# A depthwise convolution shared among four engines: four taps of two channel tiles become TensorE products with diagonal weights

## The chip, the cores and the metric

The kernel runs on one core of one Trainium2 chip. The metric is the device time of the whole program in microseconds (us). TensorE (PE in the profile) multiplies matrices and writes its sums to PSUM; VectorE (DVE), ScalarE (ACT) and GpSimd (POOL) work elementwise, and GpSimd doesn't reach PSUM; SyncE (SP) issues transfers. Each engine takes its own instructions in order and waits for others by semaphores.

## The reference, cut to what matters

A two-layer encoder on two sequences of 256 tokens with 1024 features, in fp32. Each layer has a mixer and a feed-forward part, each followed by a residual sum and a layer normalization. The first mixer is neighbourhood attention with a spatial gating unit. The second one is latent attention beside a gated convolution over time; the convolution has 31 taps, one weight per tap and channel, 512 channels:

```python
def dwconv(x, w, b):
    K, C = w.shape
    y = lax.conv_general_dilated(x, w[:, None, :].astype(x.dtype), window_strides=(1,),
                                 padding=[(K // 2, K // 2)],
                                 dimension_numbers=('NWC', 'WIO', 'NWC'),
                                 feature_group_count=C)
    return y + b.astype(x.dtype)
...
    c = latent_attention(c_q, c_kv, k_r, q_norm_g, w_uq, kv_norm_g, w_ukv, cos, sin)
    d = glu_a * jax.nn.sigmoid(glu_g)
    d = jax.nn.silu(layernorm(dwconv(d, conv_w, conv_b), conv_ln_g, conv_ln_b))
    return jnp.concatenate([c, d], axis=-1) @ w_out
```

The feed-forward part widens to 5632 features, has a convolution of three taps, gates, and narrows again to 1024.

## The kernel before, in words

The 512 tokens of both sequences are worked on together. Dense products split each fp32 operand into a rounded part and a rest ("hi" and "lo"), and take three products (hi x hi, hi x lo, lo x hi); `wload` (L105) loads a piece of weights and makes the two parts, the first on ScalarE (L109), the second on VectorE (L111). Products of plain fp32 operands, as the scores of the second mixer (`score`, L688), go to TensorE as they are; the trace has two records for each of them.

The order of the first layer is mixer, feed-forward; then comes `odd_mixer` (L532), the second mixer, and its feed-forward part. In `odd_mixer`:

- `glu(i)` (L536) makes channel tile i (of four, 128 channels each) of the convolution's input: two dense products of 24 steps each, then `gate(i)` (L546) under a raised priority. The gate takes the sigmoid on ScalarE (L551; for tiles 2 and 3 a tiny exponential behind it at L553 brings ScalarE's table for the softmax), multiplies on VectorE (L554) into `dpad[i]`, which holds both sequences with 15 zeros on either side, and begins two partial sums: `accps[i]`, a PSUM bank, with tap 0 and the bias on VectorE (L557), and `acc2`, in SBUF, with tap 21 on ScalarE (L559).
- `cproj`, `chain`, `kvproj`, `qproj` (L575 to L680) make the latent rows, normalize and transpose them (L622), and project keys, values and queries.
- `attend(p)` (L682) is attention for a pair of heads: for each sequence scores on TensorE, then for each head a maximum on VectorE (L491), exponentials with their sum on ScalarE (L494), a reciprocal on VectorE (L497), scaling (L501, on ScalarE; for the last pair L503, on VectorE), transposes on TensorE (L508), a copy out (L510), and the product with the values (L517) one step later. The exponentials lie in `er`, a `Ring` of two buffers, which makes four slots.
- L715 to L725 are the rest of the convolution. For each tile, VectorE adds taps 1 to 20 onto `accps[i]` (L719), one instruction a tap; for taps 22 to 30 ScalarE makes a scaled copy (L723, `pr`) and GpSimd adds it onto `acc2` (L724); VectorE adds the two sums at the end (L725).
- `conv_ln` (L727) transposes, normalizes over channels, transposes back (L748), applies SiLU and splits the result (L115, L116) into `mixT[4]` to `mixT[7]`; `OutProj` multiplies with the output weights, attention's half (`first`) before the convolution's half (`second`).

The order on each engine isn't the order of the code. The framework plans it from a timeline of estimated durations and priorities: what is ready and stands early in the code, or under a raised priority, goes first, and the rest of the convolution, which stands behind attention in the code, is filled in between. SBUF comes from pools with a fixed number of buffers: `act` has 30 of 4 KB per partition, `tmp` has 8; a new tile waits until a buffer is given back. PSUM has pools pA (4 banks), pB and pC (2 each). `Ring` (L77) takes `act` buffers and sets one element of each by a VectorE memset (L81).

Of the kernel before, what the change touches and what calls it, by code (L numbers as in the profile page):

```python
# [11 lines left out]
AF = mybir.ActivationFunctionType  # L12
# [3 lines left out]
P = 128  # L16
D = 1024
KC = 8
S = 256
# [4 lines left out]
RMS_EPS = 1e-6  # L24
NPAIR = 22
NPOOL = 10
NWARM = 18
ACUT = 832
KEEP = {4: 0, 7: 1, 10: 2, 13: 3}
# [20 lines left out]
def tile_encoder(ctx: ExitStack, tc: tile.TileContext, I, O):  # L50
# [26 lines left out]
    class Ring:  # L77
# [6 lines left out]
        def get(self):  # L84
            j = self.i % (2 * len(self.t))
            self.i += 1
            return self.t[j // 2][:, j % 2, :].rearrange("p (a k) -> p a k", a=2)

    def bank(pool, s="ps"):
        return pool.tile([P, 512], F32, tag="b", name=nm(s))  # L90
# [441 lines left out]
    def odd_mixer(xT):  # L532
# [13 lines left out]
        def gate(i, pa, pg):  # L546
            sg = tmp([P, 512], s="sig")
            d = dpad[i]
            out, va = d[:, :, 15:15 + S], pa.rearrange("p (s t) -> p s t", s=2)
            vs = sg.rearrange("p (s t) -> p s t", s=2)  # L550
            nc.scalar.activation(out=sg, in_=pg, func=AF.Sigmoid)  # L551
            if i >= 2:
                preload(AF.Exp, sg[:, 0:1])  # L553
            nc.vector.tensor_tensor(out=out, in0=va, in1=vs, op=ALU.mult)  # L554
            accps[i] = bank(pA, "cacc")
            a, a2 = accps[i].rearrange("p (s t) -> p s t", s=2), acc2[i // 2][:, i % 2]
            nc.vector.tensor_scalar(out=a, in0=d[:, :, 0:S], scalar1=pc("cw", i * 32),  # L557
                                    scalar2=pc("cw", i * 32 + 31), op0=ALU.mult, op1=ALU.add)
            nc.scalar.activation(out=a2, in_=d[:, :, 31 - NPOOL:31 - NPOOL + S], func=AF.Copy,  # L559
                                 scale=pc("cw", i * 32 + 31 - NPOOL))  # L560

        for i in range(4):
            d = act([P, 2, S + 30], s="dpad")
# [4 lines left out]
        for a in acc2:  # L568
            nc.gpsimd.memset(a[:, 0, 0, 0:1], 0.0)
        pr_ring = Ring(1, "pr")  # L570
        rope = const.tile([P, 2, 2, 32], F32, name="rope")
        after_mm(nc.gpsimd.dma_start(out=rope, in_=I["rope"]), last_mm[0])
        G = {"start": last_mm[0]}
# [107 lines left out]

        def attend(p):  # L682
            if p == 0:
                G["ring"] = Ring(2, "er"), Ring(2, "PTr")
            er, PTr = G["ring"]
            qT, kT = G["qT"][p], G["kT"][p]

            def score(out, qs, ks):  # L688
                for h in range(2):
                    mm(out[h], qT[:, h, qs], kT[:, h, ks], True, True)  # L690
            mixT[p] = act([P, 2, T], F32R, "mixT")
            if p == 2:
                G["sink"] = ToFeat(xscr[1], 1, last_mm[0], "ln1_g1", "ln1_b1", xscr[2], ())
            attention(p, score, G["V"], mixT[p], lambda ps, h, e: ps, er, PTr, p < 3, p == 3)
# [19 lines left out]
        op.first(0, (0, 1))  # L714
        for i in range(4):  # L715
            a, a2 = accps[i].rearrange("p (s t) -> p s t", s=2), acc2[i // 2][:, i % 2]
            for j in range(1, 31 - NPOOL):
                with tc.issue_after(G["cT_lo"].ins) if i == 0 and j >= 18 else nullcontext():
                    nc.vector.scalar_tensor_tensor(out=a, in0=dpad[i][:, :, j:j + S], scalar=pc("cw", i * 32 + j),  # L719
                                                   in1=a, op0=ALU.mult, op1=ALU.add)  # L720
            for j in range(32 - NPOOL, 31):
                pr = pr_ring.get()
                nc.scalar.activation(out=pr, in_=dpad[i][:, :, j:j + S], func=AF.Copy, scale=pc("cw", i * 32 + j))  # L723
                nc.gpsimd.tensor_tensor(out=a2, in0=a2, in1=pr, op=ALU.add)  # L724
            nc.vector.tensor_tensor(out=a2, in0=a, in1=a2, op=ALU.add)  # L725
# [196 lines left out]
```

## Time and profile before

| what | value |
|---|---|
| median of 3 runs | 1106.43 us (1104.14 to 1106.67) |
| the profiled execution | 1104.76 us, its span 1102.9 us |
| TensorE busy, span | 1082.3 us, 98% |
| VectorE busy | 673.2 us, 61% |
| ScalarE busy | 488.7 us, 44% |
| GpSimd busy | 226.6 us, 21% |
| mean granted clock of TensorE | 0.992 |

The span is what lies between the first and the last record of the profiled execution; its own time is 1.86 us longer. A busy share is an average over stages with different limits, so a stage is read from a stretch of its own. The granted clock is given as a share of 2.4 GHz.

### The profile page before, as it was taken

Reading aid. Unit: us, or ns where it says so; the run is one execution under the profiler, and the core shown is the slowest. Engines: PE = TensorE matmul, PEld = TensorE weight load, DVE = VectorE, ACT = ScalarE, POOL = GpSimd, SP = SyncE. Lnnn points to the kernel's source line nnn. Section 1 sums busy time; section 2 is a strip of 40 time slices with the busy share of each in tenths; the row PEclk is TensorE's granted clock in tenths of the full one; section 3 lists DMA queues with packets and bytes.
Section 4 is the critical chain, followed back from the end, with each engine's and each line's share of the span. In section 5 each row is a group of like instructions: output and inputs, shape, how many; then the busy total and the mean of one; then the engine's idle time right before and its main releaser. Section 6 shows DMA issues by size and latency. Waiting matters only on the chain.

```text
span 1102.9 us, 13655 instructions
## 1 busy us (share of the span) xinstructions
PE 1082.3 (98%) x5210; PEld 900.8 (82%) x5210; DVE 673.2 (61%) x996; ACT 488.7 (44%) x783; POOL 226.6 (21%) x222
## 2 busy tenths in 40 slices
PE   9999999999999999999999979999999999999996
PEld 7888778988888888888898856899888888888885
DVE  5378955766565656422578999587665656542227
ACT  5436644544444444421266797355444444431110
POOL 0482001200000000005464661830000000000173
PEclk9999999999999999999999979999999999999999
DMA  7852223533333323645232104254333333222602
GB/s 256 244 141 77 60 103 107 163 105 96 96 96 96 96 96 99 206 166 180 80 122 58 38 20 153 66 172 122 100 96 96 96 96 96 96 96 96 215 34 76
DMA packets 36098, 124.21 MB, mean 113 GB/s; under 512 B 4289, under 2 KB 5057, under 8 KB 36033
## 3 DMA queue, kind: packets, MB, share of 16 engines
q1 hardware_dynamic: 28864, 100.05, 29.5%
q0 software_dynamic: 6448, 22.53, 6.0%
q8 instruction: 41, 0.67, 0.3%
q10 hardware_dynamic: 720, 0.75, 0.2%
q14 instruction: 25, 0.20, 0.1%
HBM read 113.88 MB, written 8.39 MB: 111 GB/s over the span
## 4 chain that ended last, share of the span: by engine, by line
PE 93%; DVE 3%; ACT 2%; issue 1%; DMA 0%; POOL 0%; POOLq 0%; DVEq 0%; ACTq 0%
PE up L95 44%; PE dn L95 29%; PE qk L95 4%; PE op L95 4%; PE glu L95 3%; PE v L95 2%; PE u L95 2%; PE s L95 1%; PE pv L95 1%; PE pt L508 1%; DVE cacc L719 1%; PE lnT L237 1%; DVE wlo L111 1%; DVE qT L655 0%; ACT er L494 0%
## 5 line engine op out<-in xcount | busy, mean ns | idle before, releaser
L95 PE MATMUL up<-xT,whi 128*128 128x512 f32 (+1 forms) x1536 | 439.9, 371 | 0.0
L111 DVE TENSOR_TENSOR wlo<-raw,whi 128x1024 fp32r<-128x1024 f32 (+1 forms) x174 | 238.8, 1374 | 297.4 <-ACT whi L109 296.1
L95 PEld LDWEIGHTS up<-xT,whi 128*128 128x128 f32 x1536 | 279.9, 188 | 49.9
L109 ACT CAST whi<-raw 128x1024 fp32r<-128x1024 f32 (+1 forms) x174 | 182.4, 1050 | 249.1 <-PE dn L95 132.6
L95 PE MATMUL up<-xT,wlo 128*128 128x512 f32 (+1 forms) x768 | 284.0, 372 | 0.0
L95 PE MATMUL dn<-whi,gT 128*128 128x512 f32 x704 | 217.4, 389 | 0.0
L95 PEld LDWEIGHTS up<-xT,wlo 128*128 128x128 f32 x768 | 144.4, 188 | 24.9
L95 PEld LDWEIGHTS dn<-whi,gT 128*128 128x128 f32 x704 | 132.0, 188 | 27.2
L95 PE MATMUL dn<-wlo,gT 128*128 128x512 f32 x352 | 136.9, 389 | 0.0
L186 POOL DMA_DIRECT2D xres<-xscr x12 | 6.5, 546 | 576.0 <-PE dn L95 576.0
L95 PEld LDWEIGHTS dn<-wlo,gT 128*128 128x128 f32 x352 | 66.1, 188 | 13.8
L115 ACT CAST gT<-cv 128x512 fp32r<-128x512 f32 x44 | 27.3, 620 | 111.6 <-DVE cv L782 111.6
L771 ACT ACTIVATE cv<-up,par 128x512 f32<-128x512 f32 x88 | 68.3, 776 | 0.0
L774 DVE SCALAR_TENSOR_TENSOR cv<-up,par,cv 128x510 f32<-128x510 f32 x88 | 65.8, 748 | 2.7
L781 ACT ACTIVATE cv<-cv 128x512 f32<-128x512 f32 x44 | 27.8, 632 | 85.2 <-DVE cv L774 85.2
L772 DVE SCALAR_TENSOR_TENSOR cv<-up,par,cv 128x510 f32<-128x510 f32 x88 | 65.4, 743 | 0.0
L719 DVE SCALAR_TENSOR_TENSOR cacc<-dpad,par,cacc 128x512 f32<-128x512 f32 x80 | 58.9, 750 | 1.1
L724 POOL TENSOR_TENSOR acc<-acc,pr 128x512 f32<-128x512 f32 x36 | 48.7, 1353 | 38.9 <-ACT pr L723 32.2
L116 DVE TENSOR_TENSOR gT<-cv,gT 128x512 fp32r<-128x512 f32 x44 | 30.4, 692 | 27.5 <-ACT gT L115 27.5
L95 PE MATMUL op<-whi,mixT 128*128 128x512 f32 x128 | 44.3, 402 | 0.0
L95 PE MATMUL dn<-whi,mixT 128*128 128x512 f32 x128 | 42.8, 394 | 0.0
L95 PE MATMUL glu<-xT,khi 128*128 128x512 f32 (+1 forms) x160 | 42.0, 349 | 0.0
(195 smaller groups left out, 1351.4 us busy)
## 6 DMA issues: line engine op xcount, KB each, us to landing
raw<-in_wup SPq DMA_DIRECT2D x88, 512.0 KB, 3.6
raw<-in_wdn SPq DMA_DIRECT2D x44, 512.0 KB, 3.5
raw<-in_wout SPq DMA_DIRECT2D x16, 512.0 KB, 3.7
xscr<-xres POOLq DMA_DIRECT2D x12, 512.0 KB, 3.7
xres<-xscr POOLq DMA_DIRECT2D x12, 512.0 KB, 4.4
raw<-in_wqk SPq DMA_DIRECT2D x8, 512.0 KB, 6.6
raw<-in_wglu SPq DMA_DIRECT2D x8, 512.0 KB, 3.8
raw<-in_wug SPq DMA_DIRECT2D x7, 512.0 KB, 3.6
```

The source lines that it names most:

```text
L95: last_mm[0] = nc.tensor.matmul(out=out, lhsT=lhsT, rhs=rhs, start=first, stop=last)
L109: nc.scalar.copy(out=hi[:, :n], in_=raw[:, :n])
L111: nc.vector.tensor_tensor(out=lo[:, :n], in0=raw[:, :n], in1=hi[:, :n].bitcast(F32), op=ALU.subtract)
L115: nc.scalar.copy(out=dst[:, 0, sl], in_=src)
L116: nc.vector.tensor_tensor(out=dst[:, 1, sl], in0=src, in1=dst[:, 0, sl].bitcast(F32), op=ALU.subtract)
L237: nc.tensor.transpose(self.banks[k // 2][:, (k % 2) * S + q * P:(k % 2) * S + q * P + P], x[:, k * P:(k + 1) * P], ident)
L719: nc.vector.scalar_tensor_tensor(out=a, in0=dpad[i][:, :, j:j + S], scalar=pc("cw", i * 32 + j), in1=a, op0=ALU.mult, op1=ALU.add)
L724: nc.gpsimd.tensor_tensor(out=a2, in0=a2, in1=pr, op=ALU.add)
L771: nc.scalar.activation(out=c, in_=pv, func=AF.Identity, scale=pc(fw, ch * 4 + 1), bias=pc(fw, ch * 4 + 3))
L772: nc.vector.scalar_tensor_tensor(out=c[:, :, 1:S], in0=pv[:, :, 0:S - 1], scalar=pc(fw, ch * 4), in1=c[:, :, 1:S], op0=ALU.mult, op1=ALU.add)
L774: nc.vector.scalar_tensor_tensor(out=c[:, :, 0:S - 1], in0=pv[:, :, 1:S], scalar=pc(fw, ch * 4 + 2), in1=c[:, :, 0:S - 1], op0=ALU.mult, o ...
L781: nc.scalar.activation(out=cg, in_=cg, func=AF.Silu)
```

## The change

For channel tiles 2 and 3, taps 27 to 30 become four products on TensorE. Their weights are diagonal matrices, one for each tile and tap, in a new tile `taps` that GpSimd makes at the start of the second mixer by multiplying the identity with the taps' weights. The four products go into the bank `accps[i]` inside `gate(i)`, in place of the VectorE instruction that began this sum; tap 0 becomes one more step of VectorE's chain, and the bias moves into ScalarE's first tap, whose function is Identity with a bias instead of Copy. ScalarE and GpSimd lose four taps of each of the two tiles: 22 to 26 are left. The buffers for the exponentials of the second mixer are taken from the pool `tmp`, one at a time, instead of a ring of two `act` buffers. Tiles 0 and 1 are as before, but for the function's name at L559, which is Identity with a bias of 0.

```diff
--- before.py
+++ after.py
@@ -24,6 +24,7 @@
 RMS_EPS = 1e-6
 NPAIR = 22
 NPOOL = 10
+NTAP = 4
 NWARM = 18
 ACUT = 832
 KEEP = {4: 0, 7: 1, 10: 2, 13: 3}
@@ -85,6 +86,10 @@
             j = self.i % (2 * len(self.t))
             self.i += 1
             return self.t[j // 2][:, j % 2, :].rearrange("p (a k) -> p a k", a=2)
+
+    class Loose:
+        def get(self):
+            return tmp([P, 512], s="e").rearrange("p (a k) -> p a k", a=2)
 
     def bank(pool, s="ps"):
         return pool.tile([P, 512], F32, tag="b", name=nm(s))
@@ -554,10 +559,15 @@
             nc.vector.tensor_tensor(out=out, in0=va, in1=vs, op=ALU.mult)
             accps[i] = bank(pA, "cacc")
             a, a2 = accps[i].rearrange("p (s t) -> p s t", s=2), acc2[i // 2][:, i % 2]
-            nc.vector.tensor_scalar(out=a, in0=d[:, :, 0:S], scalar1=pc("cw", i * 32),
-                                    scalar2=pc("cw", i * 32 + 31), op0=ALU.mult, op1=ALU.add)
-            nc.scalar.activation(out=a2, in_=d[:, :, 31 - NPOOL:31 - NPOOL + S], func=AF.Copy,
-                                 scale=pc("cw", i * 32 + 31 - NPOOL))
+            if i < 2:
+                nc.vector.tensor_scalar(out=a, in0=d[:, :, 0:S], scalar1=pc("cw", i * 32),
+                                        scalar2=pc("cw", i * 32 + 31), op0=ALU.mult, op1=ALU.add)
+            else:
+                for n in range(NTAP):
+                    mm(a, taps[:, i - 2, n, :], d[:, :, 31 - NTAP + n:31 - NTAP + n + S], n == 0, n == NTAP - 1)
+            nc.scalar.activation(out=a2, in_=d[:, :, 31 - NPOOL:31 - NPOOL + S], func=AF.Identity,
+                                 scale=pc("cw", i * 32 + 31 - NPOOL),
+                                 bias=pc("cw", i * 32 + 31) if i >= 2 else 0.0)
 
         for i in range(4):
             d = act([P, 2, S + 30], s="dpad")
@@ -568,6 +578,11 @@
         for a in acc2:
             nc.gpsimd.memset(a[:, 0, 0, 0:1], 0.0)
         pr_ring = Ring(1, "pr")
+        taps = act([P, 2, NTAP, P], s="taps")
+        for i in range(2):
+            o = PCOL["cw"][0] + (i + 2) * 32 + 31 - NTAP
+            nc.gpsimd.tensor_tensor(out=taps[:, i], in0=ident[:, None, :].broadcast_to([P, NTAP, P]),
+                                    in1=par[:, o:o + NTAP, None].broadcast_to([P, NTAP, P]), op=ALU.mult)
         rope = const.tile([P, 2, 2, 32], F32, name="rope")
         after_mm(nc.gpsimd.dma_start(out=rope, in_=I["rope"]), last_mm[0])
         G = {"start": last_mm[0]}
@@ -681,8 +696,8 @@
 
         def attend(p):
             if p == 0:
-                G["ring"] = Ring(2, "er"), Ring(2, "PTr")
-            er, PTr = G["ring"]
+                G["ring"] = Ring(2, "PTr")
+            er, PTr = Loose(), G["ring"]
             qT, kT = G["qT"][p], G["kT"][p]
 
             def score(out, qs, ks):
@@ -714,11 +729,11 @@
         op.first(0, (0, 1))
         for i in range(4):
             a, a2 = accps[i].rearrange("p (s t) -> p s t", s=2), acc2[i // 2][:, i % 2]
-            for j in range(1, 31 - NPOOL):
+            for j in range(1 if i < 2 else 0, 31 - NPOOL):
                 with tc.issue_after(G["cT_lo"].ins) if i == 0 and j >= 18 else nullcontext():
                     nc.vector.scalar_tensor_tensor(out=a, in0=dpad[i][:, :, j:j + S], scalar=pc("cw", i * 32 + j),
                                                    in1=a, op0=ALU.mult, op1=ALU.add)
-            for j in range(32 - NPOOL, 31):
+            for j in range(32 - NPOOL, 31 if i < 2 else 31 - NTAP):
                 pr = pr_ring.get()
                 nc.scalar.activation(out=pr, in_=dpad[i][:, :, j:j + S], func=AF.Copy, scale=pc("cw", i * 32 + j))
                 nc.gpsimd.tensor_tensor(out=a2, in0=a2, in1=pr, op=ALU.add)
```

## Rows read from the trace of the kernel before

**Rows 1.** The page, part 1: busy us of each engine, share of the span, instructions.

```profile
PE 1082.3 (98%) x5210; PEld 900.8 (82%) x5210; DVE 673.2 (61%) x996; ACT 488.7 (44%) x783; POOL 226.6 (21%) x222
```

**Rows 2.** Stretches of the second mixer: length, busy us PE, PEld, DVE, ACT, POOL; granted clock.

```profile
612.00:641.00 29.00, 29.00 (x133) 24.14 (x133) 27.39 (x40) 21.84 (x40) 17.55 (x13) 1.00 0.19 55
630.00:641.00 11.00, 11.00 (x54) 9.25 (x53) 10.59 (x14) 7.74 (x19) 9.42 (x7) 1.00 0.33 96
641.00:660.00 19.00, 11.78 (x41) 7.28 (x40) 17.19 (x32) 18.33 (x42) 10.44 (x9) 0.64 0.01 1
644.50:658.00 13.50, 9.48 (x27) 5.53 (x28) 13.09 (x24) 13.47 (x33) 9.56 (x8) 0.50 0.01 2
660.00:682.00 22.00, 20.42 (x120) 14.50 (x119) 20.83 (x47) 20.08 (x63) 5.28 (x9) 1.00 0.46 168
682.00:742.00 60.00, 59.98 (x343) 50.32 (x342) 42.36 (x79) 26.99 (x48) 31.29 (x22) 1.00 0.34 105
```

**Rows 3.** Timeline of TensorE: start us, us, what, how often, [idle before, releaser].

```profile
638.31 0.39 PE L95 MATMUL glu<-xT,klo 128*128 128x512 f32 x1
...
640.70 0.60 PE L508 MATMUL pt<-ident,er 128*128 128x128 f32 x4
647.50 2.07 PE L95 MATMUL s<-kT,qT 128*128 128x256 f32 x4 [6.20 <-ACT er L494]
...
709.80 0.39 PE L95 MATMUL op<-whi,mixT 128*128 128x512 f32 x1
```

**Rows 4.** Groups of instructions, shapes apart, 545 to 742: count | busy us, mean ns | idle.

```profile
L719 DVE SCALAR_TENSOR_TENSOR cacc<-dpad,par,cacc 128x512 f32<-128x512 f32 x80 | 58.9, 750 | 1.1
L724 POOL TENSOR_TENSOR acc<-acc,pr 128x512 f32<-128x512 f32 x36 | 48.7, 1353 | 38.9 <-ACT pr L723 32.2 <-issue 4.9
...
L723 ACT ACTIVATE pr<-dpad,par 128x512 f32<-128x512 f32 x36 | 25.2, 723 | 5.6 <-POOL acc L724 5.6
...
L557 DVE TENSOR_SCALAR cacc<-dpad,par 128x512 f32<-128x512 f32 x4 | 3.2, 810 | 0.0
```

**Rows 5.** Timeline of VectorE, columns as in rows 3.

```profile
569.73 0.06 DVE L81 MEMSET pr<- 128x1 f32 x1 [3.26 <-PE glu L95]
...
588.38 0.55 DVE L610 TENSOR_TENSOR craw<-ra,rb 128x128 f32<-128x128 f32 x1
...
622.89 0.69 DVE L554 TENSOR_TENSOR dpad<-glu,sig 128x512 f32<-128x512 f32 x1
...
629.66 3.81 DVE L111 TENSOR_TENSOR wlo<-raw,whi 128x1024 fp32r<-128x1024 f32 x2
...
634.05 0.68 DVE L491 TENSOR_REDUCE nmx<-s 128x2 f32<-128x512 f32 x1
...
642.44 0.69 DVE L554 TENSOR_TENSOR dpad<-glu,sig 128x512 f32<-128x512 f32 x1 [1.41 <-ACT sig L551]
...
706.49 1.27 DVE L116 TENSOR_TENSOR mixT<-cb,mixT 128x512 fp32r<-128x512 f32 x2
```

**Rows 6.** Groups of ScalarE's instructions, 634 to 682, columns as in rows 4.

```profile
L723 ACT ACTIVATE pr<-dpad,par 128x512 f32<-128x512 f32 x12 | 8.5, 726 | 1.5 <-POOL acc L724 1.5
```

**Rows 7.** Chain of waits that ended last: start us, us, engine, tile, line, how often.

```profile
586.57 8.65 PE glu L95 x38
595.22 1.31 PE dn L622 x12
...
651.86 2.07 PE s L95 x4
...
660.36 0.86 PE s L95 x4
```

**Rows 8.** Timeline of GpSimd, columns as in rows 3.

```profile
575.52 4.03 POOL L724 TENSOR_TENSOR acc<-acc,pr 128x512 f32<-128x512 f32 x3 [4.86 <-issue]
```

**Rows 9.** Timeline of ScalarE in the first mixer and its output's normalization.

```profile
98.36 1.28 ACT L494 ACT_TABLE_LOAD   x1
...
185.79 3.76 ACT L246 ACTIVATE xv<-lnT,par 128x256 f32<-128x256 f32 x8
```

**Rows 10.** Timeline of ScalarE at the end of attention in the second mixer.

```profile
685.85 0.47 ACT L494 ACTIVATE er<-s,nmx 128x256 f32<-128x256 f32 x1 [3.30 <-DVE nmx L491]
```


## The prediction

> **What bounds the kernel now.** I read the page's totals first: TensorE is busy for 98% of the span, 1082.3 us [rows 1], so nearly all work added to it must find one of its few gaps. Next I cut the second mixer into stretches [rows 2]. The reader should see three stages there. From 612 to 641 us TensorE has no gap. From 641 to 660 it is busy for 11.78 of 19 us at a mean granted clock of 0.64, and from 660 to 682 for 20.42 of 22. After 682 it is full again, and the feed-forward that follows fills it to the end. So time is won or lost in this mixer by how much of TensorE's waiting between 641 and 682 remains, less what is added to its work.
>
> How large is that loss? Idle time is 7.22 + 1.58 = 8.8 us [rows 2]. From 644.5 to 658 us the granted clock is 0.50, 1.2 of 2.4 GHz, and there the engine is busy for 9.48 us [rows 2], of which half, 4.7 us, would go at the full clock. That makes 13.5 us.
>
> Who makes it wait? The gap of 6.20 us before a score product ends on ScalarE's exponential [rows 3]. From 641 to 660 ScalarE is busy for 18.33 of 19 us and from 660 to 682 for 20.08 of 22; VectorE for 17.19 and 20.83 [rows 2]. Attention is paced by ScalarE, with VectorE, which squeezes the convolution in between, close behind.
>
> **The change part by part.** *Taps taken off ScalarE and GpSimd.* Tiles 2 and 3 drop from nine scaled copies to five each. Eight copies of 0.72 us leave ScalarE and eight adds of 1.35 us, 10.8 us, leave GpSimd [rows 4]. GpSimd ends nothing here, so its relief counts for nothing; a VectorE split that runs slower beside it would gain at most tenths, since the pair at 629.66 [rows 5] still meets the adds that remain. On ScalarE only copies that stand in its full stretch count, from 634 on. Twelve stand there [rows 6], the last three of tile 2 and the nine of tile 3. Five of tile 2 and five of tile 3 stay, those of tile 2 all before 634, so of the twelve five stay and seven go. A copy's record of 0.72 us overlaps the next one by some 0.1, so I price it at 0.63, an estimate. Gain: 7 x 0.63 = 4.4 us of ScalarE.
>
> *VectorE.* The first tap of tiles 2 and 3, a TENSOR_SCALAR of 0.81 us, becomes a 0.75 us step of the chain [rows 4], and two memsets go: 0.2 us in all. The number of steps stays, 21 per tile. So VectorE is not relieved; it can only use its idle time, 1.81 us between 641 and 660 and 1.17 up to 682, and 0.41 before 641 (11.00 less 10.59, from 630 on) [rows 2], together 3.4 us. That caps the gain at 3.4 us, unless chain steps slip past the end of attention. I take the cap.
>
> *Products on TensorE.* Eight products of 512 fp32 columns. The trace has fp32 products of 256 columns: four records, which are two products, in 0.86 us at the full clock and 2.07 at half [rows 7], so 0.43 and 1.03 us each. With twice the columns a tap costs 0.86, four 3.4, eight 6.9 us at the full clock. Where do they lie? Tile 2's become ready when VectorE has made their input, about 623.6 [rows 5]; TensorE is full then, with q products and the last gated unit's, up to 638.7 [rows 3]. They push these 3.4 us later, into the gap that starts at 641. The pushed gate of tile 3 is not urgent for VectorE, which still has steps of tile 2 to do. The q products feed VectorE steps that are over when its two splits begin at 629.66; attention's first maximum comes only at 634.05, after them [rows 5]. Those 3.8 us of splits cover the push. Cost 0, and 3.4 us if the cover fails. Tile 3's four come once VectorE has made its input, 643.1 in the trace of before and a little later now. They fall into the 6.2 us gap, or delay the scores behind them: cost 0 to 3.4 us. I take 0, the gap being the nearest row. Check: 13.5 less 6.9 less 3.4 leaves 3.2 us of loss over 41 us, which is the rate of 660 to 682 (1.58 in 22). The sum is possible, but nothing larger is, without a better clock.
>
> *What waits behind a tap.* TensorE takes its queue in order, so until the gate's product on VectorE lands, scores and transposes behind the taps stand still. VectorE itself waited 1.41 us there for the sigmoid [rows 5]. That much could come on top; bound 0 to 1.4, taken 0, since TensorE idled through that wait already.
>
> *Diagonals.* Two GpSimd products over 512 columns, about 1.35 us each like the adds of that size, 2.7 us, fit the 4.86 us in which GpSimd idles before its first adds [rows 8]. They take a buffer of a full pool of thirty: the memset before them waited 3.26 us for one [rows 5]. The tile for the second sequence's latent rows, first written at 588.38 [rows 5], may then wait until half of gated unit 1 is through (24 products from 586.57 on, 0.228 each by 38 in 8.65: 592.0), 3.6 us later, and the transposes at 595.22 [rows 7], which need it, come late by at most as much. TensorE has the 48 products of gated unit 2 to do meanwhile: 0, bound 3.6. The scratch tiles for exponentials come from eight slots instead of four: 0, or a few tenths of gain.
>
> *Bias in the first ScalarE tap.* An Identity with a bias in place of Copy. Could it force a table load, 1.28 us? After the load for the exponential at 98.36 the same function with bias ran at 185.79 with no load between [rows 9]. Cost 0.
>
> *After 682.* TensorE needs the convolution's output at 709.80; VectorE's last write of it is at 707.7, 2.1 us ahead [rows 3, 5]. The transposes, ScalarE's function and these writes follow TensorE's order and move up with it, up to the cap taken. The sum: 1104.76 for the profiled execution (span 1102.9 and 1.86 around it) less 3.4 is 1101.4. The median of the runs shown stands 1.67 above that execution, so **1103.0 us** against 1106.43.
>
> **Rivals.** *VectorE holds it.* It is busy 95% of 660 to 682; its steps are as many as before, and if order and latency use up its idle time again, attention ends when it did and the eight products only fill gaps. For: the steps of cacc, 0.75 us each, stand before every maximum, and the last exponential, at 685.85, had waited 3.30 us for VectorE's [rows 10]. Against: they have no due time before the output projection. Gain 0 to 1.5, say 0.7: 1105.7.
>
> *The products stand in the way* (slower). Place: TensorE's queue, at 623.6 and 645. Price: four products 3.4 us before q, and four more between gate and scores, each time with ScalarE starved as long. It decides if attention's first scores move by more than VectorE's two splits hide, 3.8 us: from there each us of push is a us of the end. Price with relief partly kept: 6.9 less 3.4, plus 3.5 us: 1109.9. With only one burst uncovered it is 0. For: TensorE is full from 612 to 641 [rows 2]. Against: ScalarE has copies to do during the bursts.
>
> *The clock holds.* The granted clock fell to 0.50 after TensorE had stopped at 641.3, and rose again near 658, after products had run from 647.5 [rows 2, 3]. With 3.4 us of gated products pushed to 644.7 and tile 3's taps to 648.5, the long gap may not form at all, and scores, transposes and values that took twice their time would cost ScalarE less waiting: up to 4.7 us more, of which 3.2 is left to win by the check above: 1103.0 - 3.2 = 1099.8. The Trainium skill, "TensorE: Matmul & The Clock Gate", in its Part 1 says the full clock is a state that activity releases and idling takes back; by it this case would be the likeliest and the time near 1100. Here the trace agrees on the fall, but it has no stretch of mixed short products that shows the clock held. Against the rival: each tap waits for VectorE, so a gap stays before it.
>
> *It does not do what it says:* the planner may place the taps late, at the end of tile 2's chain, so that VectorE idles for them. Then 2 to 4 us are lost; I count this with the slower case.
>
> **How the numbers follow.** The sum's own case gets 0.45, and its bounds (from -5 to about -1 us) put 0.25 of that at faster and 0.20 at same. About 0.3%, 3.3 us, is what a measurement can tell from no change. The clock's case gets 0.15, all faster. VectorE's case gets 0.17, all same. The products in the way get 0.23, of which 0.20 slower and 0.03 same. Faster 0.40, same 0.40, slower 0.20. The range goes from the clock's case, 1099.5, to just short of the worst of the slower case, 1109.0: beyond it lies about a fifth.
>
> **What would show it.** Right: eight fp32 products of 512 columns near 624 to 649, records of 0.43 us apart and two per product; ten copies in place of eighteen for tiles 2 and 3; the last exponential before 683 instead of 685.85; TensorE's waits between 641 and 682 down from 8.8 to about 3 us. Wrong: a wait of TensorE on dpad longer than 1.5 us, VectorE idle in front of the chain of tile 2, first scores after 633, or the convolution's last add later than in the trace of before. The forecast fails on the good side if the clock is 1.00 all through.

## The result and the profile after

The changed kernel takes 1122.54 us (median of four runs, 1122.16 to 1124.79) against 1105.29 for the kernel before beside it: ratio 1.0167, interval 1.0155 to 1.0179. That is 17.2 us slower. The forecast was 1103.0 us with a range up to 1109.0, so both its sign and its range were wrong. The profiled execution took 1122.57 us, its span 1120.8.

The line of totals on the page of the kernel after answers to [rows 1]:

```profile
PE 1093.7 (98%) x5226; PEld 906.0 (81%) x5226; DVE 671.7 (60%) x994; ACT 484.9 (43%) x775; POOL 215.5 (19%) x216
```

TensorE is busy 11.4 us longer than before, and its idle time grows from 1102.9 - 1082.3 = 20.6 to 1120.8 - 1093.7 = 27.1 us. These 11.4 + 6.5 us are the 17.9 by which the span grew. The stretches of the kernel after show where, columns as in [rows 2]:

```profile
612.00:641.00 29.00, 29.00 (x125) 22.76 (x124) 27.54 (x40) 19.32 (x36) 11.80 (x9) 1.00 0.19 55
641.00:660.00 19.00, 14.15 (x76) 9.59 (x75) 14.16 (x28) 17.66 (x47) 0.00 (x0) 1.00 0.10 29
660.00:682.00 22.00, 21.98 (x100) 14.17 (x99) 15.43 (x30) 18.27 (x51) 9.53 (x11) 0.93 0.40 144
682.00:700.00 18.00, 16.56 (x93) 12.35 (x92) 14.82 (x31) 5.49 (x14) 0.00 (x0) 1.00 0.20 60
700.00:722.00 22.00, 16.87 (x73) 13.19 (x72) 10.75 (x21) 7.60 (x11) 16.41 (x11) 0.84 0.17 48
722.00:742.00 20.00, 20.00 (x96) 16.68 (x95) 11.96 (x26) 7.83 (x10) 6.83 (x6) 1.00 0.37 117
742.00:760.00 18.00, 14.37 (x97) 13.46 (x96) 11.45 (x31) 10.52 (x21) 9.32 (x10) 0.81 0.46 164
```

Read it against [rows 2] in two halves. From 641 to 682 the change looks like a success: TensorE waits 4.85 + 0.02 us instead of 8.8, and the granted clock is 1.00 and 0.93 where it was 0.64 in the first of the two stretches. But look at VectorE in the same lines: 14.16 of 19 and 15.43 of 22 us, where it had been busy for 17.19 and 20.83, and GpSimd has no instruction at all from 641 to 660. The engines that carry the convolution run out of work while attention runs. The bill comes after 682, where TensorE had been full: 1.44, 5.13 and 3.63 us of waiting, and a mean granted clock of 0.84 and 0.81.

Why did they run out? ScalarE's timeline of the kernel before, columns as in [rows 3]:

```profile
635.40 0.48 ACT L494 ACTIVATE er<-s,nmx 128x256 f32<-128x256 f32 x1
...
638.34 0.47 ACT L494 ACTIVATE er<-s,nmx 128x256 f32<-128x256 f32 x1
...
641.81 0.60 ACT L551 ACTIVATE sig<-glu 128x512 f32<-128x512 f32 x1
```

And ScalarE's timeline of the kernel after:

```profile
640.63 0.47 ACT L499 ACTIVATE e<-s,nmx 128x256 f32<-128x256 f32 x1 [1.99 <-DVE nmx L496]
...
644.23 0.50 ACT L499 ACTIVATE e<-s,nmx 128x256 f32<-128x256 f32 x1
...
647.34 0.46 ACT L499 ACTIVATE e<-s,nmx 128x256 f32<-128x256 f32 x1
...
650.03 0.48 ACT L499 ACTIVATE e<-s,nmx 128x256 f32<-128x256 f32 x1
...
652.49 0.45 ACT L499 ACTIVATE e<-s,nmx 128x256 f32<-128x256 f32 x1
...
655.39 0.46 ACT L499 ACTIVATE e<-s,nmx 128x256 f32<-128x256 f32 x1
...
657.24 0.60 ACT L556 ACTIVATE sig<-glu 128x512 f32<-128x512 f32 x1
```

One unit of attention (a head of a pair on one sequence) is two exponentials; the first of each is shown. Before, the sigmoid of channel tile 3 stood behind two units. After, it stands behind eight: two that start before 640, the five from 640.63 to 652.49, and the first half of the one at 655.39. Its input didn't hold it there. TensorE's timeline of the kernel after has the last record of that input (`glu`, at 644.32):

```profile
625.77 3.60 PE L100 MATMUL cacc<-dpad,taps 128*128 128x512 f32 x8
...
644.32 0.39 PE L100 MATMUL glu<-xT,klo 128*128 128x512 f32 x1
...
659.76 1.99 PE L100 MATMUL s<-kT,qT 128*128 128x256 f32 x4 [3.68 <-ACT e L499]
661.55 4.47 PE L100 MATMUL cacc<-dpad,taps 128*128 128x512 f32 x8
...
745.13 1.84 PE L100 MATMUL up<-xT,whi 128*128 128x256 f32 x5 [2.37 <-DVE xT L252]
...
748.59 0.58 PE L100 MATMUL up<-xT,whi 128*128 128x256 f32 x1 [1.18 <-POOL xT L254]
```

The gate's product was complete at 644.71, and its sigmoid began 12.5 us later because ScalarE's planned order had put attention ahead of it. Everything of tile 3 hangs behind. VectorE's timeline of the kernel before, one line:

```profile
675.18 0.69 DVE L725 TENSOR_TENSOR acc<-cacc,acc 128x512 f32<-128x512 f32 x1
```

And VectorE's timeline of the kernel after:

```profile
657.87 0.69 DVE L559 TENSOR_TENSOR dpad<-glu,sig 128x512 f32<-128x512 f32 x1 [2.91 <-ACT sig L556]
...
666.06 2.34 DVE L734 SCALAR_TENSOR_TENSOR cacc<-dpad,par,cacc 128x512 f32<-128x512 f32 x3 [1.36 <-PE cacc L100]
...
693.95 0.68 DVE L740 TENSOR_TENSOR acc<-cacc,acc 128x512 f32<-128x512 f32 x1
```

The input of tile 3 comes at 657.87 instead of 642.44 [rows 5], its chain can only start at 666.06 behind the products, and the convolution's last add comes at 693.95 instead of 675.18, 18.8 us later. Its normalization and its half of the output projection follow, TensorE runs out of other work from 700 on, and the feed-forward's first products wait for the end of the mixer (the lines at 745.13 and 748.59). In the kernel before, the first of them ran without a wait:

```profile
731.54 0.76 PE L95 MATMUL up<-xT,whi 128*128 128x256 f32 x5
```

GpSimd's timeline of the kernel after shows the same hole, and the price of the diagonals above it:

```profile
569.34 2.05 POOL L584 TENSOR_TENSOR taps<-ident,par 128x512 f32<-128x512 f32 x2 [0.67 <-PE glu L100]
...
575.00 4.02 POOL L739 TENSOR_TENSOR acc<-acc,pr 128x512 f32<-128x512 f32 x3 [2.19 <-issue]
...
661.68 1.27 POOL L739 TENSOR_TENSOR acc<-acc,pr 128x512 f32<-128x512 f32 x1 [27.17 <-ACT pr L738]
```

The diagonals delay nothing on GpSimd: the adds behind them begin at 575.00, against 575.52 [rows 8]. Then GpSimd waits 27.17 us for a scaled copy of tile 3.

### The profile page after: what moved, and what is told of

Read it like the earlier page. It is cut to its first block, busy times and chain, and to the rows that moved or that the text cites. A ratio compares the mean times of both kernels' runs of the same rounds, so it can differ in the third digit from the quotient of the medians.

```text
span 1120.8 us, 13672 instructions
## 1 busy us (share of the span) xinstructions
PE 1093.7 (98%) x5226; PEld 906.0 (81%) x5226; DVE 671.7 (60%) x994; ACT 484.9 (43%) x775; POOL 215.5 (19%) x216
## 4 chain that ended last, share of the span: by engine, by line
PE 93%; DVE 3%; ACT 1%; POOL 1%; issue 1%; DMA 0%; POOLq 0%; DVEq 0%; ACTq 0%
PE up L100 43%; PE dn L100 28%; PE qk L100 4%; PE glu L100 4%; PE op L100 4%; PE v L100 2%; PE u L100 2%; PE s L100 1%; PE pv L100 1%; PE q L100 1%; PE pt L513 1%; PE lnT L242 1%; DVE cacc L734 1%; DVE wlo L116 1%; PE cacc L100 1%
## 5 line engine op out<-in xcount | busy, mean ns | idle before, releaser
L734 DVE SCALAR_TENSOR_TENSOR cacc<-dpad,par,cacc 128x512 f32<-128x512 f32 x82 | 61.6, 752 | 2.9 <-PE cacc L100 1.4
L739 POOL TENSOR_TENSOR acc<-acc,pr 128x512 f32<-128x512 f32 x28 | 38.0, 1357 | 55.1 <-ACT pr L738 51.4
```

## The experiments

The theory: **the place of tile 3's sigmoid in ScalarE's planned order decides**, by way of the end of the convolution. The main rival: the products themselves, on TensorE, are the cost. A second group of runs asks which engine paces attention, on which the forecast's gain rested. All runs in one table; "behind" counts the attention units planned ahead of tile 3's sigmoid. The times of single instructions are from one profiled execution each; "last exponential" is the start of its second half (before: 686.32, where [rows 10] has the first half, at 685.85). Each ratio is taken against executions of the kernel before beside that run, whose medians lie between 1104.32 and 1105.29; differences in us below are taken against those.

| run | sigmoid behind | sigmoid at | last add | last exponential | us, median | ratio to before, interval |
|---|---|---|---|---|---|---|
| before | 2 | 641.81 | 675.18 | 686.32 | 1105.29 | |
| after | 8 | 657.24 | 693.95 | 686.94 | 1122.54 | 1.0167 (1.0155 to 1.0179) |
| e1_ring | 4 | 647.39 | 680.88 | 683.93 | 1111.92 | 1.0067 (1.0050 to 1.0084) |
| e2_loose_only | 8 | 657.67 | 688.74 | 688.20 | 1114.48 | 1.0091 (1.0076 to 1.0106) |
| e3_glu3_early | 4 | 647.18 | 682.43 | 684.33 | 1110.04 | 1.0052 (1.0037 to 1.0067) |
| e4_ring_tile3 | 2 | 642.08 | 677.43 | 684.38 | 1104.35 | 0.9996 (0.9987 to 1.0006) |
| e5_ring_tile2 | 4 | 646.76 | 679.53 | 684.66 | 1105.68 | 1.0013 (1.0004 to 1.0022) |
| e6_tile3_dve_taps | 2 | 642.54 | 674.39 | 686.27 | 1109.09 | 1.0048 (1.0031 to 1.0064) |
| e7_loose_mid | 2 | 641.44 | 674.16 | 682.94 | 1104.21 | 0.9998 (0.9988 to 1.0007) |
| e8_all_mid | 2 | 645.21 | 677.84 | 686.34 | 1106.00 | 1.0010 (1.0001 to 1.0019) |
| e9_ring_mid | 2 | 645.50 | 678.17 | 686.71 | 1106.17 | 1.0013 (1.0004 to 1.0022) |
| e10_affine_late | 2 | 642.76 | 674.61 | 686.50 | 1104.48 | 1.0000 (0.9992 to 1.0009) |
| e11_8dve_late | 2 | 642.54 | 670.05 | 686.45 | 1104.67 | 1.0000 (0.9992 to 1.0009) |
| e12_tile3_two | 2 | 642.78 | 676.88 | 685.39 | 1105.16 | 1.0004 (0.9995 to 1.0013) |
| e13_both_eight | 2 | 642.18 | 673.86 | 684.98 | 1104.58 | 1.0002 (0.9993 to 1.0011) |
| e14_both_four | 2 | 642.19 | 675.46 | 683.99 | 1103.90 | 0.9996 (0.9987 to 1.0005) |

### Which part of the change costs

**e1_ring**: the whole change, with the ring for the exponentials put back.

```diff
-                G["ring"] = Ring(2, "PTr")
-            er, PTr = Loose(), G["ring"]
+                G["ring"] = Ring(2, "er"), Ring(2, "PTr")
+            er, PTr = G["ring"]
```

> The changed kernel with one part undone: the second mixer's exponentials lie in the ring of two buffers again; products, diagonals and bias as changed. In its order of instructions the sigmoid of tile 3 stands behind four units of attention, where the changed kernel has eight and the kernel before two. Theory A, the late sigmoid (tile 3's convolution starts 16 us late because the scratch tiles let attention run ahead, and the convolution's half of the output then starves TensorE): 1101 to 1107 us, convolution's last add near 676. Theory B, the eight products and the diagonals themselves cost the time: 1117 us or more, whatever the buffers.

**e2_loose_only**: the kernel before with nothing changed but those two lines, the other way round (and the class `Loose`); no products.

> The kernel before with the scratch tiles for the exponentials alone: no products, no diagonals. Its sigmoid of tile 3 stands behind eight units of attention. Theory A: the loss is there without any product, 1114 to 1123 us (less TensorE work than the changed kernel by 6.9 us, but four more copies and adds behind the late gate). Theory B: 1104 to 1107 us, as before.

The two lines alone cost 9.6 us (1114.48 against 1104.90), with no tap on TensorE at all, and their sigmoid stands behind eight units at 657.67, as in the kernel after. With the ring put back, 7.0 us of the 17.2 remain. So the part that seemed neutral carries more than half of the loss. The products are not innocent: e1's 1111.92 lies between the ranges of its two theories, and its sigmoid still slips to behind four units.

What is it in the two lines? The ring holds four tiles, the pool `tmp` has eight buffers, so attention may run further ahead. But `gate` takes the sigmoid's own tile from `tmp` as well (`sg = tmp([P, 512], s="sig")`), so the exponentials' tiles now stand in one row with it. In every run with loose tiles the sigmoid stands behind just those units whose tiles the code takes from `tmp` before it: eight in the kernel after and in e2, where `glu(3)` follows two pairs, four in e3, two in e7, e8 and e12. With the ring and `glu(3)` in its old place, behind eight units in the code, it stands behind two or four. That speaks for the shared pool, handed out in the order of the code, rather than for the number of buffers. No run gives the exponentials eight buffers of their own, so it isn't shown.

**e4_ring_tile3** and **e5_ring_tile2**: the ring, and products for one tile only. The edit of e4 against the kernel after, cut; e5 has `PT = (2,)`, and the other tests on `i` change in the same way:

```diff
+PT = (3,)
...
-            if i < 2:
+            if i not in PT:
```

> Ring as before, products for tile 3 alone (tile 2 keeps its VectorE start and all nine copies). Sigmoid behind two units, as in the kernel before. Theory A: four products fall into TensorE's gap after the gate: 1102 to 1106 us, clock perhaps higher than 0.50 near 650. Theory B: half of the loss, 1111 to 1115 us.

> Ring as before, products for tile 2 alone (tile 3 as before). Sigmoid of tile 3 behind four units. Theory A, stated closer after the first four runs: VectorE is full from 612 to 682, so what it does for attention it does not do for the convolution; the time follows the end of tile 3's convolution, and that follows tile 3's sigmoid. Tile 2's products push the last gated unit on a full TensorE, so 1107 to 1112 us with the sigmoid 4 to 6 us late. Theory B (the number of products counts, wherever they stand): like tile 3 alone, 1104 to 1105 us.

Tile 3's products alone leave the sigmoid at 642.08 and the time as it was. Tile 2's alone push it to 646.76, behind four units: their 3.60 us stand ahead of the rest of tile 3's gated unit in TensorE's queue, as the line at 625.77 shows for the kernel after. There the convolution still ends at 679.53, and the ratio of 1.0013 is 1.4 us. The sigmoid came as late as e5's first theory said, but the time didn't: it had 1107 us or more.

### The place of the sigmoid

**e3_glu3_early** calls `glu(3)` one attention pair earlier in the code; **e7_loose_mid** and **e8_all_mid** call it inside the first pair, between its two sequences. e7 has the loose tiles and no products (so it is e2 but for the call), e8 the whole change (so it is the kernel after but for the call). Each instruction is still there. The edit of e7 and e8, cut:

```diff
+            if s == 1 and mid is not None:
+                mid()
...
+        G["mid"] = lambda: glu(3)
         attend(0)
         attend(1)
-        glu(3)
```

> The whole change, scratch tiles too, with one line moved: the gated unit of tile 3 stands between the first and the second pair of heads in the code, not behind the second. The sigmoid then stands behind four units of attention. Theory A: the place of the sigmoid is what costs, so 1101 to 1108 us with everything else of the change in it. Theory B: 1117 us or more. A third one, that scratch tiles cost by themselves (buffers shared with other scratch tiles): above 1110 us here and near 1104 with the ring.

> The kernel before with scratch tiles for the exponentials, and the gated unit of tile 3 called from inside the first pair's attention, between its two sequences, so that the sigmoid stands behind two units again. No products. Theory A: the scratch tiles cost nothing once the sigmoid is in its old place: 1103 to 1107 us. Theory C (they cost by themselves, by sharing buffers with other scratch tiles): 1111 us or more, as with the scratch tiles alone.

> The whole change, with the gated unit of tile 3 called from inside the first pair's attention, as in the run before it; sigmoid behind two units. Theory A: most of the 17 us are gone; tile 2's products still push the last gated unit by 3.4 us, so 1103 to 1108 us and better than with the unit behind the first pair (1110.0). Theory B: 1117 us or more.

e3 moved the sigmoid only to behind four units, and 5.1 us of loss stay, more than its first theory allowed. e7 and e8 put it behind two. The loose tiles then cost nothing: e7 at 1104.21 against e2 at 1114.48, with the same operations in the code. And the whole change costs 1.3 us where it had cost 17.2. The move carries all of tile 3's gated unit, not the sigmoid alone, and the plan around it moves too, so what is shown is that this unit's place in the plan is worth 17.2 - 1.3 = 15.9 us.

**e9_ring_mid** is e8 with the ring.

> Whole change with the ring of exponentials' tiles kept, and tile 3's gated unit called inside the first pair's attention, so that its sigmoid stands behind two attention units in ScalarE's planned order instead of four. Theory (the sigmoid's place in ScalarE's order decides, through the end of tile 3's convolution): sigmoid near 642 to 646 us, last add of the convolution 676 to 680, TensorE full from 722 to 760, time 1103 to 1107. Rival (the four extra products per tile are the cost, wherever the sigmoid stands): last add stays above 680, 1110 to 1113 as with the ring and the old call.

1106.17 against e1's 1111.92: with the ring too, the unit's place decides, and ring and loose tiles then make no difference (1106.17 and 1106.00).

But with the ring it is another engine that makes the sigmoid late. TensorE's timeline of e1, the last record of `glu`:

```profile
645.14 0.39 PE L100 MATMUL glu<-xT,klo 128*128 128x512 f32 x1
```

And ScalarE's timeline of e1:

```profile
646.09 1.28 ACT L556 ACT_TABLE_LOAD   x1
...
647.39 0.60 ACT L556 ACTIVATE sig<-glu 128x512 f32<-128x512 f32 x1
```

ScalarE turns to the sigmoid's table 0.56 us after the product, so it isn't ScalarE's order that holds it. The product itself ends at 645.53 instead of 638.70 [rows 3]: 3.60 us of tile 2's products, and 3.2 us of attention's scores and transposes that TensorE's order now has between the last steps of `glu`. The same holds in e3 and e5. Only in the kernel after and in e2 does the sigmoid stand long behind a product that is done, 12.5 and 19.0 us. So the theory is right on the gate's place in the plan, and on ScalarE's order only for the loose tiles.

How the loss grows isn't even. Leaving out e6, which the next section explains, it is at most 1.9 us up to a last add near 679.5; at 680.88 (e1) it is already 7.0, and at 682.43 (e3) 5.1. The stretches of e1, columns as in [rows 2], show what is late:

```profile
700.00:722.00 22.00, 21.11 (x98) 17.11 (x97) 11.24 (x13) 7.93 (x11) 15.02 (x6) 1.00 0.22 62
722.00:742.00 20.00, 15.64 (x85) 13.54 (x84) 15.61 (x41) 12.50 (x20) 9.37 (x11) 0.91 0.56 195
```

And TensorE's timeline of e1:

```profile
734.26 0.74 PE L100 MATMUL up<-xT,whi 128*128 128x256 f32 x4 [2.26 <-DVE xT L252]
```

TensorE is full from 700 to 760 in e4, e5, e7 and e8; in e1 it waits 4.36 us between 722 and 742. By then the products that do not need the convolution are used up, and what follows the output projection, the normalization and its transposes, lies bare.

### A collision on the way

**e6_tile3_dve_taps**: ring, tile 3 only, and taps 17 to 20, which are VectorE's, as products in place of ScalarE's and GpSimd's 27 to 30. Its edit against the kernel before, cut:

```diff
+PE_TAPS = [17, 18, 19, 20]
+NTAP = len(PE_TAPS)
+PT = (3,)
...
+                for n, j in enumerate(PE_TAPS):
+                    mm(a, taps[:, n, :], d[:, :, j:j + S], n == 0, n == NTAP - 1)
...
+                if i in PT and j in PE_TAPS:
+                    continue
```

> Ring, products for tile 3 alone, but of taps 17 to 20, which are VectorE's, instead of 27 to 30; ScalarE and GpSimd keep all nine copies. Theory A: VectorE's chain for tile 3 has 17 steps instead of 21, the convolution ends some 3 us earlier than with tile 3's other products: 1100 to 1103.5 us. Rival of my prediction (ScalarE's copies pace attention and with it the time): the copies are back, so 1105 to 1108 us.

The convolution ends earlier than before, at 674.39, and yet the time is 1109.09. That speaks against the theory as I had put it, so the cause had to be found. VectorE's timeline of e6:

```profile
686.36 0.58 DVE L510 TENSOR_SCALAR er<-er,ri 128x256 f32<-128x256 f32 x2
...
688.30 4.77 DVE L510 TENSOR_SCALAR er<-er,ri 128x256 f32<-128x256 f32 x2
```

And GpSimd's timeline of e6:

```profile
688.19 9.44 POOL L201 TENSOR_TENSOR xres<-xres,rowg 128x1024 f32<-128x1024 f32 x4
```

One pair of scalings takes 0.58 us at 686.36, the next, of the same shape, 4.77 at 688.30. The convolution's normalization, done earlier, had released GpSimd's products on the residual, which began 0.11 us before the pair; each lasts 9.44 / 4 = 2.36 us, and two of them are 4.72, just the time of the pair. The Trainium skill, "SBUF — State Buffer", section "Who interferes with whom", says that VectorE and GpSimd share a pair of ports as a lock, that a tensor_scalar can enter a mode that needs it, and that whoever comes second stands still until the other's instruction is done. The trace agrees: about one GpSimd product of 2.36 us for each scaling.

**e10_affine_late** makes GpSimd's products wait for the last scaling:

```diff
-                        sink.res.affine(range(NT))
+                        sink.res.affine(range(NT), last_sc[0])
```

> The kernel with taps 17 to 20 of tile 3 as products, in which GpSimd's products on the residual wait for the last VectorE scaling of the exponentials. Theory (VectorE's scalings stood long because GpSimd's products ran beside them): the last pair of scalings takes 0.6 to 0.8 us instead of 4.77, TensorE's busy time from 682 to 700 rises from 14.83 to 16.5 or more of 18, time 1103 to 1106.5 against 1109.1. Rival (the early end of the convolution or the products themselves cost it, and the long records are only where a wait shows): scalings still above 2 us or the time stays at 1108 to 1110.

VectorE's timeline of e10:

```profile
688.52 0.60 DVE L511 TENSOR_SCALAR er<-er,ri 128x256 f32<-128x256 f32 x2
```

And GpSimd's timeline of e10:

```profile
689.21 10.41 POOL L201 TENSOR_TENSOR xres<-xres,rowg 128x1024 f32<-128x1024 f32 x4 [0.75 <-DVE er L511]
```

The pair is back at 0.60 us, TensorE is busy for 17.85 of the 18 us from 682 to 700 (14.83 in e6), and 4.6 us of time are gone (1109.09 to 1104.48). The collision was e6's whole loss. The theory holds with this proviso: a convolution that ends early helps nothing if it sets GpSimd loose on VectorE's last scalings.

### What paces attention

The forecast took ScalarE for the pace. e11 to e14 have the convolution's end at or near its old place, and free different engines. **e11_8dve_late** is e10 with `PE_TAPS` 13 to 20 (VectorE loses eight steps). **e12_tile3_two** is e8 with `NTAP = 2` and tile 3 alone. **e13_both_eight** is e10 with taps 17 to 20 and 27 to 30, **e14_both_four** with 19, 20, 29 and 30 (VectorE, ScalarE and GpSimd each lose four, or two).

> Eight of VectorE's taps of tile 3 (13 to 20) as products, the nine scaled copies kept, ring kept, GpSimd's residual products behind the last scaling. VectorE loses eight steps of 0.75 us, 6 us; TensorE gains eight products, 6.9 us. Theory (VectorE paces attention from 641 to 682, but TensorE is short by only some 13 us there): last add 667 to 672, last exponential 680 to 684, and the time 1100 to 1105, as half or more of the relief is eaten by the products. Rival (the end of the convolution no longer decides once it lies before 679, and products are net cost): 1105 to 1110.

> Two products in place of eight: taps 29 and 30 of tile 3 alone, loose scratch tiles, tile 3's gated unit called inside the first pair's attention so that its sigmoid stands behind two units. Theory 1 (the granted clock is held by the short burst of fp32 products in TensorE's gap, however few): granted clock 1.00 from 641 to 660 us, some 4.7 us of half-clock time won for 1.8 us of products, time 1100.5 to 1103, faster than before. Theory 2 (what is won in clock comes from four or more products, the gap shortened by them): clock 0.7 to 0.9 there, sum of idle, slow time and products as before, time 1103.5 to 1106, no difference. Either way the last add of the convolution lies at 673 to 678.

> Tile 3 alone, eight products: taps 17 to 20 (VectorE's) and 27 to 30 (ScalarE's and GpSimd's), ring kept, residual products behind the last scaling. TensorE has the same eight products as in the run with VectorE's taps 13 to 20; VectorE loses four steps (3.0 us), ScalarE four copies (2.5 us). Theory 1 (ScalarE and VectorE pace attention together): last exponential 682.5 to 685 instead of 686.45, time 1100 to 1103, faster than before. Theory 2 (neither: the round of a unit and TensorE's added work fill whatever is freed): last exponential 686 to 687, time 1104 to 1106.

> The same with four products: taps 19, 20, 29 and 30 of tile 3. VectorE loses two steps (1.5 us), ScalarE two copies (1.3 us), TensorE gains 3.5 us. Theory 1 (paced together): last exponential 684 to 685.5, time 1101.5 to 1103.5. Theory 2: last exponential 685.5 to 687, time 1104 to 1105.5, no difference from before.

None differs from before by what can be measured. The stretches of e8, columns as in [rows 2]:

```profile
641.00:660.00 19.00, 15.35 (x71) 9.96 (x70) 16.11 (x29) 16.75 (x39) 6.35 (x5) 1.00 0.00 1
660.00:682.00 22.00, 19.51 (x110) 13.16 (x110) 20.64 (x41) 19.77 (x59) 3.21 (x6) 1.00 0.47 168
682.00:742.00 60.00, 59.75 (x339) 50.05 (x338) 46.20 (x87) 27.18 (x46) 33.67 (x24) 1.00 0.32 98
```

The same stretches of e11:

```profile
641.00:660.00 19.00, 16.23 (x62) 9.20 (x61) 16.27 (x27) 18.45 (x41) 9.85 (x8) 0.91 0.01 1
660.00:682.00 22.00, 20.57 (x122) 14.25 (x121) 20.72 (x49) 20.34 (x64) 7.05 (x12) 1.00 0.46 168
682.00:742.00 60.00, 59.65 (x338) 50.29 (x337) 38.09 (x72) 26.66 (x46) 30.60 (x20) 1.00 0.33 106
```

The first stretch of e12:

```profile
641.00:660.00 19.00, 12.39 (x52) 7.50 (x50) 17.18 (x31) 18.63 (x44) 8.99 (x8) 0.91 0.01 1
```

The first two stretches of e13:

```profile
641.00:660.00 19.00, 15.63 (x67) 9.54 (x67) 16.50 (x29) 17.48 (x40) 9.51 (x11) 1.00 0.19 62
660.00:682.00 22.00, 20.34 (x119) 14.28 (x120) 21.09 (x48) 19.48 (x62) 1.13 (x2) 1.00 0.32 115
```

The first two stretches of e4:

```profile
641.00:660.00 19.00, 14.22 (x66) 8.39 (x66) 16.65 (x30) 18.64 (x45) 9.53 (x11) 1.00 0.15 51
660.00:682.00 22.00, 19.48 (x110) 13.70 (x109) 21.33 (x44) 18.25 (x56) 0.00 (x0) 1.00 0.33 125
```

And of e14:

```profile
641.00:660.00 19.00, 13.76 (x59) 7.68 (x60) 16.64 (x30) 18.97 (x45) 9.16 (x8) 1.00 0.01 1
660.00:682.00 22.00, 20.16 (x119) 14.33 (x116) 20.63 (x46) 18.98 (x60) 3.28 (x7) 1.00 0.46 168
```

Add up what TensorE loses from 641 to 742, idle time and half-clock time, together with the products it was given. Before: 13.5 us, no products. e8: 6.39 idle, 7.28 of products (3.60 and 3.68), no half clock: 13.7. e11: 4.55 idle and 8.81 of products (eight, partly at the half clock): 13.4. In these two the sum stays where it was, and the time within 1.3 us. But the sum doesn't settle it. e13, which relieves both engines, comes to 5.05 (with 0.02 idle after 682) and 7.12, 12.2. e4 and e14, with four products at the full clock (3.68), have 7.67 and 7.33 of idle time (0.37 and 0.25 of it after 682), 11.4 and 11.0 in all, some 2 us less than before; yet none of the three medians differs from before.

The last exponential did move where copies left ScalarE and nothing was pushed: 685.39 with two copies gone (e12), 684.38 with four (e4), 683.99 and 684.98 with steps of VectorE gone too (e14, e13). Where VectorE alone lost steps it stayed: 686.50 and 686.45 (e10, e11), against e11's first theory. But the time didn't follow: e13's last exponential is inside what its first theory expected, its median of 1104.58 inside the second's; e14's 1103.90 lies between the two. e7, with nothing removed, ended attention at 682.94, the earliest of all, for no gain. So the end of attention isn't what the time follows, and relief of ScalarE, of VectorE or of both, paid for with products, gains nothing that can be measured here: the lowest end of an interval, 0.9987 (e4, e14), would be 1.4 us.

In e12, with two products (1.96 us), the mean granted clock from 641 to 660 is 0.91 instead of 0.64, but TensorE is idle for 6.61 us there, against 7.22 before, and nothing is won, much as the second theory had it. No version beats the kernel before beyond the interval; the best two, e4 and e14, are at 0.9996.

## Why the prediction was wrong

**The step that failed** is in the paragraph on the diagonals: "The scratch tiles for exponentials come from eight slots instead of four: 0, or a few tenths of gain." I priced buffers as something that is waited for, and so more of them as harmless. In a kernel whose order is planned, the pool that a tile comes from also changes the order: with the loose tiles, attention's eight units stand ahead of tile 3's sigmoid on ScalarE instead of two. e2 measured this step at +9.6 us. Whether the number of buffers does it or the pool that the exponentials now share with the sigmoid's tile is not shown; the counts speak for the pool.

**The second failed step** is "The pushed gate of tile 3 is not urgent for VectorE, which still has steps of tile 2 to do." VectorE did have such steps, but the gate was urgent for the end of the convolution. And the push is larger than the 3.4 us of the products: attention's scores and transposes came between the pushed steps on TensorE, and the gate's last product landed 6.8 us later in e1, 6.0 in the kernel after. I had asked who waits for the products, and hadn't asked which instructions overtake the ones that are pushed. In e1, with the ring, this step measured +7.0 us; with the sigmoid behind two units (e8, e9) the push costs 1.3 to 1.9 us.

With these two, the path was wrong: "The transposes, ScalarE's function and these writes follow TensorE's order and move up with it". The convolution's last add came 18.8 us later though attention ended when it did before (686.94 against 686.32), and it was the convolution that the end of the mixer waited for.

**The gain didn't show.** "Attention is paced by ScalarE" gave 4.4 us, capped by VectorE at 3.4. The seven copies went, and ScalarE answered in part with idle time (e8: 16.75 of 19 us). The runs show that with four copies off ScalarE the last exponential comes 1.9 us earlier (e4), and the time doesn't change by anything that can be measured. So the pace may have been right in part; that the time follows the end of attention was wrong.

**What held.** A tap costs 3.60 / 4 = 0.90 us at the full clock, against the 0.86 worked out from the scores. The diagonals took 2.05 us, less than the 2.7 assumed, inside GpSimd's idle time. The buffer they take did delay the second sequence's latent rows, as the prediction allowed for: they were first written at 592.58 instead of 588.38, and the transposes that need them ran 1.1 us later, but TensorE had other work and lost 0.1 us. Where the sigmoid kept its place, the products did fall into TensorE's waits almost for free, as "cost 0" said.

**The rivals.** "The clock holds" was right on the clock: 1.00 and 0.93 from 641 to 682 in the kernel after, 1.00 over both stretches in e8. The time it promised, 1099.8, didn't come even in e8, where the products and the remaining waits add up to what the half clock and the waits had cost. The Trainium skill, "TensorE: Matmul & The Clock Gate", Part 1, has the full clock as a state that activity releases and idling loses; the trace agrees in both directions, with 1.00 in e8, whose products stand in the gap, and 0.84 in the kernel after from 700 to 722, where its new waits lie. "The products stand in the way" was right on the sign and on the place in TensorE's queue, but not on its route, later first scores: they came 0.65 us later, well inside the 3.8 that it called covered, and the first exponential ran at 634.10, earlier than 635.40. "It does not do what it says" came nearest: the planner did put something late, but the gate in front of the products, and for 17 us instead of 2 to 4. Of the signs named beforehand, "the convolution's last add later than in the trace of before" was the one that came true.

What stays open: why the planner puts eight units ahead of a sigmoid with a raised priority, since a trace shows only the order that it chose, and the run that would separate the two readings (eight buffers in a pool of their own) is missing; why the loss jumps between e5 (last add 679.53, about 1 us) and e1 (680.88, 7.0 us); and what the time follows once the convolution ends early enough, when it is neither the end of attention nor the sum of TensorE's losses.

## What to carry to other kernels

Where an order is planned from estimates, price every change of a tile's pool, of a buffer count or of an earlier instruction's length by asking what may now overtake what, and then look in the new trace first for the one instruction that moved most against its inputs. Find the stage's latest chain (here gate, convolution, normalization) and protect its head in the order before giving it cheaper links. A stretch that improves, as 641 to 682 did here, proves nothing until the chain that ends after it has been followed.

## What the runs showed of the hardware that was not expected

Two fp32 scalings of 128x256 from SBUF to SBUF on VectorE took 4.77 us beside GpSimd's products of 128x1024 and 0.58 to 0.60 us without them (e6, e10), about one GpSimd product of waiting each. And the mean granted clock from 641 to 660 changed with few products in TensorE's gap: it was 0.64 before and 0.73 in e7, both without products, 0.91 with two (e12, 1.96 us), and with four 1.00 in e4 (3.68 us) but 0.91 in e10, whose four ran partly at the half clock (5.37 us). So the number of products alone doesn't tell which level a stretch gets.
